# A second quarter of the MLP's second layer by Strassen's seven products, on the same four PSUM banks

## The chip, the core and the metric

The kernel runs on one core of one Trainium2 chip. The metric is the device time of one execution in microseconds, less being better; 2064.8 us is the median of three runs before the change (2063.86 to 2065.09).

## The reference, cut to what matters

One layer of a hybrid encoder trunk on 256 tokens with 2048 features: two token mixers, a cross-attention, a squared-ReLU MLP with 8192 hidden units, and a final RMSNorm. The change touches the MLP's second layer, the product with `w_ff2`.

```python
D_MODEL = 2048; SEQ = 256; D_FF = 4 * D_MODEL
...
    h = rms_norm(x, norm_ffn_g[l])
    x = x + jnp.square(jax.nn.relu(h @ w_ff1[l])) @ w_ff2[l]
return rms_norm(x, norm_final_g)
```

## The kernel before, in words

All matrix products are made to nearly fp32 precision from three products of rounded parts: a weight tile `raw` that a DMA brings is rounded by ScalarE (ACT) to `whi`, VectorE (DVE) makes the remainder `wlo = raw - whi`, and TensorE (PE) multiplies hi by hi, hi by lo and lo by hi. Activations are kept as such pairs as well (a `Quad` `q` holds four K-tiles of 128 hidden units for all 256 tokens).

The MLP runs in four feature blocks (`fb` 0 to 3) of 2048 hidden units. In a block, `blocks` computes the first layer in eight steps `b2` of 256 hidden units (256 columns of `w_ff1`; two transfers of 1 MB each), and after each second step one of the block's four quads `hid[q]` is complete. The second layer then adds the block's share to the result `res` (2 row tiles of 128 tokens, 2048 columns, here four quarters `n` of 512 columns). Quarters 1, 2 and 3 are made by `chunk`: four pieces, one for each quad `q`, each with one 1 MB transfer of a 512 x 512 piece of `w_ff2`, its `whi`/`wlo` in two halves, and 24 matmuls of 512 columns; the two PSUM banks `s0`, `s1` are added to `res` when the fourth piece is done (L1098).

Quarter 0 is made by Strassen's scheme (`seven_products`, L1014 to L1043): a 512 x 512 piece of weights is taken as two K-halves `i`, each with four sub-blocks of 128 x 256. DVE forms sums of the sub-blocks (`tt`, L1021 to L1023); ACT and DVE make the hi and lo parts of seven matrices for one half (`sh`, `sl`, L1029 and L1030); PE multiplies them with seven combinations of the hidden units (`q` itself or the sums `cm` that `mixes` makes) in 21 matmuls of 256 columns (L1041 to L1043). The seven results stay in four PSUM banks (`seven`, tile name `b`) over all four quads and all four blocks. After the last, `unmix` copies the banks to `pc` and DVE adds them to quarter 0 of `res`.

The buffers matter here. `raw` has three buffers, shared by classical and seven-product pieces. `whi` and `wlo` have four each (two pieces). `sh` and `sl` have one each: the second half of a piece can be written only when PE has read the first.

Within an engine the instructions run in the order of the built program. A scheduler makes that order from the program's order and from priorities: transfers and the making of `whi`, `wlo`, `tt`, `sh`, `sl` have a high one, so they stand early; the rest follows as its inputs are due. All weight transfers are issued from SP's queue, in its order, each when its `raw` buffer is free.

Of the kernel before, what the change touches and what calls it, by code (L numbers as in the profile page):

```python
# [50 lines left out]
def trunk(ctx: ExitStack, tc: tile.TileContext, x, mem, positions, norm_mix_g, w_in, conv_w, gdn_a_log, gdn_dt_bias,  # L51
# [67 lines left out]

    def chunk(quads, pieces_of, evac, before=None, hold=None, between=None):  # L120


# [4 lines left out]
        held = {q: fetch(pieces_of(q), 4, 512, hold=hold) for q in ((2, 3) if hold else ())}

        def products(q, i, part, halves):
            t, c0, c1, o = part  # L130
# [4 lines left out]
            pe.matmul(o, xh, wl, start=False, stop=False)  # L135
            pe.matmul(o, xl, wh, start=False, stop=last)  # L136
# [876 lines left out]

    def seven_products(both, cm, src, first, last):  # L1014

        raw = wp.tile([P, 2048], F32, name="raw", tag="raw", bufs=3)
        rv = raw.rearrange("p (i x c) -> p i x c", i=2, x=4)
        tt = fp.tile([P, 2, 4, 256], F32, name="tt", tag="tt", bufs=1)
        with tc.high_priority(offset=100000):
            nc.sync.dma_start(raw.rearrange("p (k n) -> p k n", k=4), src.rearrange("(k p) n -> p k n", p=P))  # L1020
            vec.tensor_add(tt[:, :, 0:2, :], rv[:, :, 0:1, :].to_broadcast([P, 2, 2, 256]), rv[:, :, 1:3, :])  # L1021
            vec.tensor_add(tt[:, :, 2, :], tt[:, :, 1, :], rv[:, :, 1, :])
            vec.tensor_add(tt[:, :, 3, :], tt[:, :, 2, :], rv[:, :, 3, :])  # L1023
        for i in range(2):
            with tc.high_priority(offset=100000):
                sh, sl = (fp.tile([P, 7 * 256 + ROOM], F32R, name=n, tag=n, bufs=1)[:, SHIFT:SHIFT + 7 * 256]
                          .rearrange("p (x c) -> p x c", x=7) for n in ("sh", "sl"))
                for xs, src in ((slice(0, 3), rv[:, i, 1:4, :]), (slice(3, 7), tt[:, i])):
                    act.activation(sh[:, xs, :], src, AF.Copy)  # L1029
                    vec.tensor_sub(sl[:, xs, :], src, sh[:, xs, :].bitcast(F32))  # L1030
# [13 lines left out]

    def unmix():

        pc = fp.tile([P, 8, 256], F32, name="pc", tag="tt", bufs=1)
        for g in range(4):
            n = 2 if g < 3 else 1
            act.activation(pc[:, 2 * g:2 * g + n, :], seven[g].rearrange("p (a c) -> p a c", a=2)[:, :n, :], AF.Copy)  # L1050
        c12, c11, c22, c21 = (res[:, t, c * 256:(c + 1) * 256] for t in range(NT) for c in range(2))
# [14 lines left out]
    for fb in range(4):  # L1066
        hid, mixed = [], []

        def strassen(q):
            seven_products(hid[q].both, mixed[q], w_ff2[0, fb * D + q * 512:fb * D + (q + 1) * 512, 0:512],  # L1070
                           fb == 0 and q == 0, fb == 3 and q == 3)

        for b2 in range(8):
            if b2 % 2 == 0:
                hid.append(quad_a())
                hs = fp.tile([P, 4, S], F32, name="hs", tag="hs", bufs=2)
            at = slice(b2 % 2 * 2, b2 % 2 * 2 + 2)
# [15 lines left out]
        for n in range(1, 4):
            ns = slice(n * 512, (n + 1) * 512)
# [6 lines left out]
            def evac_o(t, ps, c0, c1):  # L1101
                got = add(t, ps, 0, 512)
                if fb == 3:
                    square_sum(ssq4[:, t, n:n + 1], got)
                    vec.tensor_mul(got, got, gfin[:, ns])

            def evac_last(t, ps, c0, c1):
# [18 lines left out]
                if t == 0:  # L1126
                    vec.tensor_mul(res[:, t, ns], res[:, t, ns], gfin[:, ns])
                for c in (0, 3, 1, 2):
                    cs = slice(c * 512, (c + 1) * 512)
                    o = res[:, t, cs]  # L1130
                    if t and c == 3:
                        vec.scalar_tensor_tensor(o, o, r, gfin[:, cs], op0=ALU.mult, op1=ALU.mult)
# [24 lines left out]

# [26 lines left out]
```

## Time and profile before

| | |
|---|---|
| median of three runs | 2064.8 us |
| the profiled execution's own time | 2066.05 us |
| its span in the profile | 2064.3 us |
| the MLP's blocks 0, 1 and 2 (1419.20 to 1592.66 and the next two) | 173.46, 173.43, 173.44 us |
| the rest of the last block and the end (from 1939.53) | 124.77 us |
| DVE busy in a block of 173.46 us | 122.45 us |
| ACT busy in it | 90.69 us |
| mean granted TensorE clock | 0.999 |

The profile is of one execution; its span lies 1.75 us under that execution's own time, which in turn is 1.25 us over the median of the runs. Busy times of an engine are the union of its instructions' times. A matmul's recorded time overlaps that of the next one, so its pace is read from start to start. "Idle before" is time in which the engine waited for the named instruction or transfer. All stretches are in microseconds from the start of the span.

### The profile page before, as it was taken

The numbers are of one execution on the slowest core, as the hardware profiler recorded it, in microseconds if no ns is written. First come the engines' busy times: TensorE is split into PE (matmuls) and PEld (weight loads), VectorE is DVE, ScalarE is ACT, GpSimd is POOL, SyncE is SP. The second block draws the span as 40 slices with busy tenths as digits, with TensorE's granted clock in tenths as the row PEclk, the third lists the DMA queues.
The fourth block names the chain that finished last, engine by engine and source line by source line (L and its number), as shares of the span: only waits on it lengthen the run. The fifth ranks groups of instructions, "written<-read, shape, count | busy, mean of one in ns | idle before, by whom it ended". The sixth has DMA issues, their size and how long they took to land.

```text
span 2064.3 us, 29089 instructions
## 1 busy us (share of the span) xinstructions
PE 2045.1 (99%) x11240; PEld 1774.0 (86%) x11240; DVE 1510.3 (73%) x2381; ACT 1132.2 (55%) x1669; POOL 26.9 (1%) x37
## 2 busy tenths in 40 slices
PE   8999999999999999999999999999999999999998
PEld 6888888888888888888888898888888888988887
DVE  6785888588957896688767665768758756775885
ACT  7564664556445644565456555555546545554664
POOL 0000000000000000000000000000000000000000
PEclk9999999999999999999999999999999999999999
DMA  8797655465556555655567664565656566656653
GB/s 302 229 313 233 207 192 199 164 208 181 198 183 199 183 195 189 189 182 180 189 192 234 194 193 147 182 189 181 224 184 198 179 204 194 194 194 195 192 198 129
DMA packets 328313, 408.28 MB, mean 198 GB/s; under 512 B 31200, under 2 KB 236528, under 8 KB 328048
## 3 DMA queue, kind: packets, MB, share of 16 engines
q1 hardware_dynamic: 328032, 405.92, 61.0%
q8 instruction: 88, 1.44, 0.3%
q10 hardware_dynamic: 144, 0.52, 0.1%
q14 instruction: 49, 0.40, 0.1%
HBM read 391.19 MB, written 15.22 MB: 197 GB/s over the span
## 4 chain that ended last, share of the span: by engine, by line
PE 97%; DMA 1%; SPq 1%; issue 0%; DVE 0%; ACT 0%; POOLq 0%; POOL 0%; DVEq 0%; ACTq 0%
PE s L172 34%; PE s L174 17%; PE s L135 12%; PE s L134 12%; PE s L136 12%; PE b L1041 1%; PE b L1042 1%; PE b L1043 1%; PE b L689 1%; DMA xc<-x 1%; PE b L590 1%; PE b L104 0%; PE b L105 0%; PE b L106 0%; SPq L290 0%
## 5 line engine op out<-in xcount | busy, mean ns | idle before, releaser
L94 DVE TENSOR_TENSOR wlo<-raw,whi 128x1024 fp32r<-128x1024 f32 x668 | 816.0, 1223 | 412.6 <-ACT whi L93 405.7
L93 ACT ACTIVATE whi<-raw 128x1024 fp32r<-128x1024 f32 x668 | 706.6, 1060 | 689.1 <-PE s L172 331.2
L172 PE MATMUL s<-q,whi 128*128 128x512 f32 x3072 | 959.7, 392 | 2.2 <-DVE bo L187 2.1
L174 PEld LDWEIGHTS s<-q,wlo 128*128 128x128 f32 x3072 | 575.3, 188 | 123.6
L174 PE MATMUL s<-q,wlo 128*128 128x256 f32 x3072 | 611.9, 280 | 0.0
L172 PEld LDWEIGHTS s<-q,whi 128*128 128x128 f32 x3072 | 468.8, 188 | 5.2 <-DVE bo L187 2.5
L134 PE MATMUL s<-whi,q 128*128 128x512 f32 x1136 | 443.6, 392 | 0.7 <-ACT whi L93 0.7
L135 PE MATMUL s<-wlo,q 128*128 128x512 f32 x1136 | 443.5, 390 | 0.6 <-DVE wlo L94 0.6
L136 PE MATMUL s<-whi,q 128*128 128x512 f32 x1136 | 441.8, 390 | 0.0
L135 PEld LDWEIGHTS s<-wlo,q 128*128 128x128 f32 x1136 | 213.9, 188 | 43.5 <-DVE wlo L94 1.1
L134 PEld LDWEIGHTS s<-whi,q 128*128 128x128 f32 x1136 | 213.7, 188 | 42.9 <-ACT whi L93 1.1
L136 PEld LDWEIGHTS s<-whi,q 128*128 128x128 f32 x1136 | 213.3, 188 | 42.8 <-DVE q L257 0.2
L541 DVE SCALAR_TENSOR_TENSOR acc<-bo,cw,acc 128x255 f32<-128x255 f32 (+1 forms) x144 | 61.3, 479 | 3.3 <-ACT acc L538 3.0
L1029 ACT ACTIVATE sh<-raw 128x768 fp32r<-128x768 f32 x32 | 27.1, 847 | 49.1 <-DMA raw<-w_ff 32.5
L187 DVE TENSOR_TENSOR bo<-bo,s 128x256 f32<-128x256 f32 x128 | 47.9, 415 | 0.0
L649 DVE TENSOR_TENSOR pr<-lw,tw 32x31 f32<-32x31 f32 (+15 forms) x124 | 40.2, 324 | 8.7 <-DMA lw<-scr_l 7.1
L651 DVE TENSOR_TENSOR tw<-tw,pr 32x31 f32<-32x31 f32 (+15 forms) x124 | 40.5, 327 | 2.2
L186 ACT ACTIVATE bo<-s 128x256 f32<-128x256 f32 x128 | 41.0, 370 | 0.0
L1030 DVE TENSOR_TENSOR sl<-tt,sh 128x1024 fp32r<-128x1024 f32 x32 | 39.1, 1223 | 0.0
L1029 ACT ACTIVATE sh<-tt 128x1024 fp32r<-128x1024 f32 x32 | 33.6, 1051 | 8.4 <-DVE tt L1023 8.4
L1043 PE MATMUL b<-sh,cm 128*128 128x256 f32 x128 | 35.5, 279 | 0.0
L1042 PE MATMUL b<-sl,cm 128*128 128x256 f32 x128 | 35.5, 279 | 0.0
(359 smaller groups left out, 1575.5 us busy)
## 6 DMA issues: line engine op xcount, KB each, us to landing
raw<-w_in SPq DMA_DIRECT2D x143, 1024.0 KB, 5.1
raw<-w_ff SPq DMA_DIRECT2D x128, 1024.0 KB, 5.8
raw<-w_xkv SPq DMA_DIRECT2D x31, 1024.0 KB, 6.4
raw<-w_out SPq DMA_DIRECT2D x16, 1024.0 KB, 5.9
raw<-w_xq SPq DMA_DIRECT2D x16, 1024.0 KB, 5.4
raw<-w_xo SPq DMA_DIRECT2D x16, 1024.0 KB, 5.4
dec_d<-dec_w SPq DMA_DIRECT2D x8, 384.0 KB, 7.9
dec<-dec_d SPq DMA_DIRECT2D x8, 384.0 KB, 4.2
```

The source lines that it names most:

```text
L93: act.activation(hi, src, AF.Copy)
L94: vec.tensor_sub(lo, src, hi.bitcast(F32))
L134: pe.matmul(o, xh, wh, start=first, stop=False)
L135: pe.matmul(o, xh, wl, start=False, stop=False)
L136: pe.matmul(o, xl, wh, start=False, stop=last)
L172: pe.matmul(ps[b], wh[:, b * P:(b + 1) * P], xhl, start=kk == 0, stop=False)
L174: pe.matmul(ps[b][:, :S], wl[:, b * P:(b + 1) * P], xh, start=False, stop=kk == KT - 1)
L187: vec.tensor_add(o, o, ps[b][:, :S])
L541: vec.scalar_tensor_tensor(acc[:, d:], ps[:, :S - d], cw[:, j, blk:blk + 1], acc[:, d:], op0=ALU.mult, op1=ALU.add)
L1029: act.activation(sh[:, xs, :], src, AF.Copy)
L1042: pe.matmul(o, lhs[0], sl[:, x, :], start=False, stop=False)
L1043: pe.matmul(o, lhs[1], sh[:, x, :], start=False, stop=last and i == 1 and (m % 2 == 1 or m == 6))
```

## The change

In blocks 0, 1 and 2, quarter 1 is made by the seven products too; its classical chunk falls away there. In block 3 quarters 1 to 3 stay classical. Both quarters use the same four banks in turn: in each of the blocks 0 to 2 the banks gather quarter 0 over the block's four quads, are copied out, cleared and added to `res` (`unmix(0, True)`), and then gather quarter 1, with a second `unmix(1, True)`. So `unmix` runs seven times in place of once. The pieces are hung behind the classical pieces of quarters 2 and 3 by a new argument `behind` of `chunk`. S(q,n) names the seven-product piece of quad q in quarter n, C(n,q) a classical piece. The program's order is: S(0,0), S(1,0) in the first layer as before, then S(2,0); C(2,0), S(3,0), C(2,1), unmix, C(2,2), S(0,1), C(2,3), S(1,1); C(3,0), C(3,1), S(2,1), C(3,2), S(3,1), C(3,3), unmix.

Beside this, `cm` has four buffers in place of two, `hs` one in place of two, one of the four sums is written back into `raw`, and the final gain (1 MB, broadcast to all partitions) is loaded in block 3 in two halves into buffers of `cb` and `hs` rather than before the MLP. The banks are cleared by ACT (a copy with scale 0), not by DVE.

```diff
-    def chunk(quads, pieces_of, evac, before=None, hold=None, between=None):
+    def chunk(quads, pieces_of, evac, before=None, hold=None, between=None, behind={}):
...
+                for f in behind.get(q, ()):
+                    f()
...
+    def clear():
+        for g in range(4):
+            act.activation(seven[g].rearrange("p (a c) -> p a c", a=4), ident.unsqueeze(1).to_broadcast([P, 4, P]),
+                           AF.Copy, scale=0.0)
...
-        cm = fp.tile([P, 2, 2, 4, P], F32R, name="cm", tag="cm", bufs=2)
+        cm = fp.tile([P, 2, 2, 4, P], F32R, name="cm", tag="cm", bufs=4)
...
-            vec.tensor_add(tt[:, :, 2, :], tt[:, :, 1, :], rv[:, :, 1, :])
-            vec.tensor_add(tt[:, :, 3, :], tt[:, :, 2, :], rv[:, :, 3, :])
+            vec.tensor_add(rv[:, :, 0, :], tt[:, :, 1, :], rv[:, :, 1, :])
+            vec.tensor_add(tt[:, :, 2, :], rv[:, :, 0, :], rv[:, :, 3, :])
...
-                for xs, src in ((slice(0, 3), rv[:, i, 1:4, :]), (slice(3, 7), tt[:, i])):
+                for xs, src in ((slice(0, 4), rv[:, i]), (slice(4, 7), tt[:, i])):
...
-    def unmix():
+    def unmix(n, again):
...
+            if again:
+                clear()
...
-                hs = fp.tile([P, 4, S], F32, name="hs", tag="hs", bufs=2)
+                hs = fp.tile([P, 4, S], F32, name="hs", tag="hs", bufs=1)
...
-        if fb == 3:
-            strassen(2)
-        for n in range(1, 4):
+        strassen(2)
+        if fb == 3:
+            load_gfin()
+        for n in range(1 if fb == 3 else 2, 4):
...
             chunk(hid, cols(w_ff2[0, fb * D:(fb + 1) * D, :], n * 512), evac_last if last else evac_o,
-                  hold=quad_b if last else None)
-            if n < 3 and fb < 3:
-                strassen(n + 1)
+                  hold=quad_b if last else None,
+                  behind=({} if fb == 3 else
+                          {0: (step(3, 0),), 1: (lambda: unmix(0, True),), 2: (step(0, 1),), 3: (step(1, 1),)} if n == 2 else
+                          {1: (step(2, 1),), 2: (step(3, 1),)}))
+            if n == 3 and fb < 3:
+                unmix(1, True)
```

How the built order changes is shown at three places of block 0. The numbers in names tell buffers' uses apart.

On SP's queue, in the second layer: L83 fetches a classical piece, L1020 (before) and L1035 (after) a seven-product piece. Before, from the last piece of quarter 1 to the piece after quarter 2:

```order
L83 DMA raw_14026<-w_ff2 128x4x512
L1020 DMA raw_14062<-w_ff2 128x4x512
L83 DMA raw_14124<-w_ff2 128x4x512
L83 DMA raw_14158<-w_ff2 128x4x512
L83 DMA raw_14192<-w_ff2 128x4x512
L83 DMA raw_14226<-w_ff2 128x4x512
L1020 DMA raw_14262<-w_ff2 128x4x512
```

After, from C(2,2) (raw_14130) to C(3,2) (raw_14450); raw_14164 is S(0,1), raw_14224 C(2,3), raw_14258 S(1,1), raw_14322 and raw_14356 C(3,0) and C(3,1), raw_14390 S(2,1):

```order
L83 DMA raw_14130<-w_ff2 128x4x512
L1035 DMA raw_14164<-w_ff2 128x4x512
L83 DMA raw_14224<-w_ff2 128x4x512
L1035 DMA raw_14258<-w_ff2 128x4x512
L83 DMA raw_14322<-w_ff2 128x4x512
L83 DMA raw_14356<-w_ff2 128x4x512
L1035 DMA raw_14390<-w_ff2 128x4x512
L83 DMA raw_14450<-w_ff2 128x4x512
```

Seven-product pieces now stand between the classical ones with one or two of these between them, where four stood before.

On DVE, before, around the end of a classical chunk (L1098 adds its two banks to `res`) and the two halves of a seven-product piece (`sl_14069` the first, `sl_14096` the second):

```order
L94 TENSOR_TENSOR wlo_14127<-raw_14124,whi_14126 128x1024
L1030 TENSOR_TENSOR sl_14069<-tt_14063,sh_14068 128x1024
L94 TENSOR_TENSOR wlo_14131<-raw_14124,whi_14130 128x1024
L94 TENSOR_TENSOR wlo_14161<-raw_14158,whi_14160 128x1024
L1098 TENSOR_TENSOR res_10093<-s0_13922,res_10093 128x512
L1098 TENSOR_TENSOR res_10093<-s1_13923,res_10093 128x512
L94 TENSOR_TENSOR wlo_14165<-raw_14158,whi_14164 128x1024
L1030 TENSOR_TENSOR sl_14096<-raw_14062,sh_14095 128x768
L1030 TENSOR_TENSOR sl_14096<-tt_14063,sh_14095 128x1024
```

After, at the end of n=2's chunk (L1120 is the add, `wlo_14325` and `wlo_14329` are C(3,0), L1071 and L1072 the recombination), and then at S(0,1) (`sl_14171`, `sl_14198`) and S(1,1) (`tt_14259`, `sl_14265`), up to C(3,2)'s first `wlo`:

```order
L1071 TENSOR_TENSOR pc_14110<-pc_14110 128x256
L1072 TENSOR_TENSOR res_10093<-res_10093,pc_14110 128x256
L94 TENSOR_TENSOR wlo_14325<-raw_14322,whi_14324 128x1024
L1120 TENSOR_TENSOR res_10093<-s0_13980,res_10093 128x512
L94 TENSOR_TENSOR wlo_14329<-raw_14322,whi_14328 128x1024
L1120 TENSOR_TENSOR res_10093<-s1_13981,res_10093 128x512
```

```order
L1045 TENSOR_TENSOR sl_14171<-raw_14164,sh_14170 128x1024
L1045 TENSOR_TENSOR sl_14171<-tt_14165,sh_14170 128x768
L1045 TENSOR_TENSOR sl_14198<-raw_14164,sh_14197 128x1024
L1045 TENSOR_TENSOR sl_14198<-tt_14165,sh_14197 128x768
L1036 TENSOR_TENSOR tt_14259<-raw_14258 128x2x512
L1037 TENSOR_TENSOR raw_14258<-tt_14259,raw_14258 128x2x256
L1038 TENSOR_TENSOR tt_14259<-raw_14258 128x2x256
L1045 TENSOR_TENSOR sl_14265<-raw_14258,sh_14264 128x1024
L1045 TENSOR_TENSOR sl_14265<-tt_14259,sh_14264 128x768
L94 TENSOR_TENSOR wlo_14453<-raw_14450,whi_14452 128x1024
```

Before, classical work stood between the two halves of a piece; now both halves and the start of the next piece follow each other, and the add of a chunk stands ahead of the second `wlo` of the next chunk's first piece.

On PE, before, behind the last products of a first half (L1041 to L1043) comes a classical piece (L134 to L136):

```order
L1042 MATMUL b_13000<-sl_14069,cm_13657 128x256
L1043 MATMUL b_13000<-sh_14068,cm_13657 128x256
L134 MATMUL s0_14122<-whi_14126,q_13006 128x512
L135 MATMUL s0_14122<-wlo_14127,q_13006 128x512
L136 MATMUL s0_14122<-whi_14126,q_13006 128x512
```

After, behind the last products of S(0,1)'s first half (L1056 to L1058, `sh_14170`):

```order
L1057 MATMUL b_12998<-sl_14171,cm_13197 128x256
L1058 MATMUL b_12998<-sh_14170,cm_13197 128x256
L1056 MATMUL b_12995<-sh_14197,q_13004 128x256
L1056 MATMUL b_12996<-sh_14197,cm_13197 128x256
L1056 MATMUL b_12997<-sh_14197,cm_13197 128x256
L1056 MATMUL b_12998<-sh_14197,cm_13197 128x256
L1057 MATMUL b_12995<-sl_14198,q_13004 128x256
```

The second half (`sh_14197`, in the same buffer as `sh_14170`) follows at once, its four products that need `sh` alone first.

More of the change, by code (lines that the diff above doesn't have):

```diff
@@ L998, in trunk, with load_gfin, final_gain @@
     seven = [bank() for _ in range(4)]
-    for g in range(4):
-        vec.memset(seven[g], 0.0)
+    gfin = []
+    def load_gfin():
+        for i, tag in enumerate(("cb", "hs")):
+            g = fp.tile([P, 1024], F32, name="gfin", tag=tag, bufs=1)
+            nc.sync.dma_start(g, norm_final_g[i * 1024:(i + 1) * 1024].partition_broadcast(P))
+            gfin.append(g)
+    def final_gain(c0, c1):
+        return gfin[c0 // 1024][:, c0 % 1024:c0 % 1024 + c1 - c0]
+    def clear():
[3 more added lines that the diff above has]
+    clear()
     def mixes(hs):
@@ L1017, in seven_products @@
         rv = raw.rearrange("p (i x c) -> p i x c", i=2, x=4)
-        tt = fp.tile([P, 2, 4, 256], F32, name="tt", tag="tt", bufs=1)
+        tt = fp.tile([P, 2, 3, 256], F32, name="tt", tag="tt", bufs=1)
         with tc.high_priority(offset=100000):
@@ L1036, in mix @@
                 return [cm[:, e, i, x, :] for e in range(2)]
-            for m, (lhs, x) in enumerate(((own(0, 0), 0), (own(1, 0), 2), (mix(3), 1), (own(1, 1), 6), (mix(1), 3),
-                                          (mix(2), 5), (mix(0), 4))):
+            for m, (lhs, x) in enumerate(((own(0, 0), 1), (own(1, 0), 3), (mix(3), 2), (own(1, 1), 6), (mix(1), 4),
+                                          (mix(2), 0), (mix(0), 5))):
                 o = seven[m // 2][:, m % 2 * 256:m % 2 * 256 + 256]
@@ L1043, in seven_products @@
                 pe.matmul(o, lhs[1], sh[:, x, :], start=False, stop=last and i == 1 and (m % 2 == 1 or m == 6))
-    def unmix():
[L1047 to L1051, printed above, removed]
+    def unmix(n, again):
+        pc = fp.tile([P, 7, 256], F32, name="pc", tag="tt", bufs=1)
+        with tc.high_priority(offset=50000):
+            for g in range(4):
+                m = 2 if g < 3 else 1
+                act.activation(pc[:, 2 * g:2 * g + m, :], seven[g].rearrange("p (a c) -> p a c", a=2)[:, :m, :], AF.Copy)
+            if again:
+                clear()
+        c12, c11, c22, c21 = (res[:, t, n * 512 + c * 256:n * 512 + (c + 1) * 256] for t in range(NT) for c in range(2))
         p1, p2, p3, p4, p5, p6, p7 = (pc[:, m, :] for m in range(7))
@@ L1067, in trunk, with strassen, step @@
         hid, mixed = [], []
-        def strassen(q):
-            seven_products(hid[q].both, mixed[q], w_ff2[0, fb * D + q * 512:fb * D + (q + 1) * 512, 0:512],
-                           fb == 0 and q == 0, fb == 3 and q == 3)
+        def strassen(q, n=0):
+            seven_products(hid[q].both, mixed[q], w_ff2[0, fb * D + q * 512:fb * D + (q + 1) * 512, n * 512:(n + 1) * 512],
+                           q == 0, q == 3)
+        def step(q, n):
+            return lambda: strassen(q, n)
         for b2 in range(8):
@@ L1104, in evac_o @@
                     square_sum(ssq4[:, t, n:n + 1], got)
-                    vec.tensor_mul(got, got, gfin[:, ns])
+                    vec.tensor_mul(got, got, final_gain(n * 512, n * 512 + 512))
             def evac_last(t, ps, c0, c1):
@@ L1126, in evac_last @@
                 if t == 0:
-                    vec.tensor_mul(res[:, t, ns], res[:, t, ns], gfin[:, ns])
+                    vec.tensor_mul(res[:, t, ns], res[:, t, ns], final_gain(n * 512, n * 512 + 512))
                 for c in (0, 3, 1, 2):
@@ L1131, in evac_last @@
                     if t and c == 3:
[L1132 removed]
+                        vec.scalar_tensor_tensor(o, o, r, final_gain(c * 512, c * 512 + 512), op0=ALU.mult, op1=ALU.mult)
                     elif t and c == 2:
@@ L1151, in trunk @@
             if fb == 3 and n == 2:
-                unmix()
+                unmix(0, False)
                 for t in range(NT):
@@ L1155, in trunk @@
                     square_sum(ssq4[:, t, 0:1], got)
-                    vec.tensor_mul(got, got, gfin[:, 0:512])
+                    vec.tensor_mul(got, got, final_gain(0, 512))
 _INS = ["x", "mem", "positions", "norm_mix_g", "w_in", "conv_w", "gdn_a_log", "gdn_dt_bias", "ret_gn_g", "gdn_norm_g",
```

2 lines of the change are left out of this document (removed).

## The prediction, made before the changed kernel was run

> **What bounds the kernel now.** I read the page first: its busy line and its chain say who sets the end. In the chain line every share is time on the path to the end.
>
> ```profile
> span 2064.3 us, 29089 instructions
> PE 2045.1 (99%) x11240; PEld 1774.0 (86%) x11240; DVE 1510.3 (73%) x2381; ACT 1132.2 (55%) x1669; POOL 26.9 (1%) x37
> PE 97%; DMA 1%; SPq 1%; issue 0%; DVE 0%; ACT 0%; POOLq 0%; POOL 0%; DVEq 0%; ACTq 0%
> ```
>
> TensorE sets the end. The view of stretches then gives one feature block of the MLP (columns: length, then busy time of PE, PEld, DVE, ACT, POOL, granted clock, DMA share, GB/s), and the view of lines in that block gives the prices.
>
> ```profile
> 1419.20:1592.66 173.46, 173.46 (x970) 151.46 (x969) 122.45 (x140) 90.69 (x108) 0.00 (x0) 1.00 0.61 194
> 1592.66:1766.09 173.43, 173.43 (x969) 151.43 (x969) 122.70 (x139) 90.94 (x108) 0.00 (x0) 1.00 0.60 194
> L94 DVE TENSOR_TENSOR wlo<-raw,whi 128x1024 fp32r<-128x1024 f32 x56 | 68.5, 1224 | 43.5 <-ACT whi L93 43.0
> L93 ACT ACTIVATE whi<-raw 128x1024 fp32r<-128x1024 f32 x56 | 59.2, 1058 | 64.1 <-PE s L136 27.5 <-PE s L172 27.2 <-DMA raw<-w_ff 9.3
> L1030 DVE TENSOR_TENSOR sl<-tt,sh 128x1024 fp32r<-128x1024 f32 x8 | 9.8, 1223 | 0.0
> L1029 ACT ACTIVATE sh<-tt 128x1024 fp32r<-128x1024 f32 x8 | 8.4, 1053 | 2.3 <-DVE tt L1023 2.3
> L1030 DVE TENSOR_TENSOR sl<-raw,sh 128x768 fp32r<-128x768 f32 x8 | 7.6, 952 | 1.0 <-ACT sh L1029 1.0
> L1029 ACT ACTIVATE sh<-raw 128x768 fp32r<-128x768 f32 x8 | 6.8, 847 | 13.5 <-DMA raw<-w_ff 9.7 <-PE b L1043 3.8
> L1021 DVE TENSOR_TENSOR tt<-raw 128x1024 f32<-128x1024 f32 x4 | 4.9, 1224 | 6.2 <-DMA raw<-w_ff 6.2
> L1098 DVE TENSOR_TENSOR res<-s,res 128x512 f32<-128x512 f32 x6 | 3.8, 682 | 0.0
> L1022 DVE TENSOR_TENSOR tt<-tt,raw 128x512 f32<-128x512 f32 x4 | 2.7, 683 | 0.0
> ```
>
> PE is busy for all of a block. ACT mostly waits for PE (64.1 us), so buffers are full and the weights are early; but 9.3 + 9.7 + 6.2 us are already waits for a weight transfer.
>
> **What PE saves.** Start times of matmuls give their real pace, since a busy time overlaps the next one.
>
> ```profile
> 1479.72 0.39 PE L135 MATMUL s<-wlo,q 128*128 128x512 f32 x1
> ...
> 1481.31 0.39 PE L136 MATMUL s<-whi,q 128*128 128x512 f32 x1
> 1481.54 0.28 PE L1042 MATMUL b<-sl,q 128*128 128x256 f32 x1
> ...
> 1483.77 0.28 PE L1043 MATMUL b<-sh,cm 128*128 128x256 f32 x1
> ```
>
> Seven steps of 512 columns take 1.59 us, 0.227 each; nineteen of 256 take 2.23, 0.117 each. A classical piece (4 K-tiles x 2 row tiles x 3) is 24 x 0.227 = 5.45 us, a seven-product piece 2 x 21 x 0.117 = 4.91. Twelve pieces change (three blocks, four quads): 12 x 0.54 = 6.5 us less PE.
>
> **What is added off PE.** Per piece, DVE does 2 x (1.22 + 0.95) + 1.22 + 2 x 0.68 = 6.9 us instead of 2 x 1.22 = 2.4, ACT 2 x 1.90 = 3.8 instead of 2.1. Per block two recombinations come on top.
>
> ```profile
> L1050 ACT ACTIVATE pc<-b 128x512 f32<-128x512 f32 (+1 forms) x4 | 2.0, 535 | 0.1
> L1054 DVE TENSOR_TENSOR res<-res,pc 128x256 f32<-128x256 f32 x1 | 0.4, 426 | 0.0
> ```
>
> Each is 4 x 0.54 on ACT, four clears of a bank that I price the same, and 11 x 0.42 = 4.6 us on DVE. A block's DVE goes from 122.5 to 122.5 + 4 x 4.5 + 9.2 - 2 x 0.68 = 148 us of about 171: no bound over the block. But from the start of n=2 to the end of its chunk (four classical pieces, three seven-product ones, one recombination, two adds) DVE needs 4 x 2.4 + 3 x 6.9 + 4.6 + 1.4 = 36.3 us and PE 4 x 5.45 + 3 x 4.91 = 36.5. No reserve builds up there. The half with four of the seven matrices first, cm in four buffers, hs in one (its next write comes a whole b2, 11 us, later), the clear on ACT, and the gain vector loaded in block 3 in two halves I cost at 0: no PE row waits for them; the cover of the last is the two raw buffers ahead, and without it 1 MB, 4.9 us, would show.
>
> **The one pair sh/sl and the three raw buffers.** These rows price a hand-over from the first half of a piece to its second, and a transfer.
>
> ```profile
> 1510.50 0.28 PE L1043 MATMUL b<-sh,cm 128*128 128x256 f32 x1
> ...
> 1510.82 0.85 ACT L1029 ACTIVATE sh<-raw 128x768 fp32r<-128x768 f32 x1 [1.41 <-PE b L1043]
> ...
> 1511.70 0.96 DVE L1030 TENSOR_TENSOR sl<-raw,sh 128x768 fp32r<-128x768 f32 x1 [1.03 <-ACT sh L1029]
> ...
> 1512.65 1.23 DVE L1030 TENSOR_TENSOR sl<-tt,sh 128x1024 fp32r<-128x1024 f32 x1
> DMA to landing us min/median/max: 4.9/5.8/5.9
> 1485.14 0.37 SPq L83 DMA_DIRECT2D raw<-w_ff  x1
> 1486.01 0.37 SPq L1020 DMA_DIRECT2D raw<-w_ff  x1
> 1492.90 1.23 DVE L1021 TENSOR_TENSOR tt<-raw 128x1024 f32<-128x1024 f32 x1 [0.76 <-DMA raw<-w_ff]
> 1510.69 2.36 SPq L83 DMA_DIRECT2D raw<-w_ff  x2
> ```
>
> sh is rewritten 0.32 us after the last matmul of the half starts, and sl 0.88 after that. A transfer takes 4.9 (alone) to 5.9 us, and 6.9 when another was issued 0.9 before it (1486.01 to 1492.90). The seven-product raw issued at 1486.01 is held until the second half's sl has read it (1512.66), 27 us. Before, one is held at a time and classical pieces cycle on two buffers. In the order after, raw_14164 and raw_14258, the next two seven-product pieces, are fetched ahead of raw_14322 and raw_14356 (n=3's first two classical pieces) and held together, so classical pieces cycle on one. And PE has nothing between the halves of S(0,1), nor between it and S(1,1) (S(q,n): quad q, quarter n; C(n,q): classical piece).
>
> **The sum of the waits.** I follow the order through one block; E is where PE starts C(3,0), and I work with cross-engine hand-overs of 0.05.
> 1. C(3,1). raw_14322 can go when S(3,0)'s second half has read its raw: that half's predecessor ends on PE 9.9 us before E (24 + 9 matmuls and a half of 2.46 stand between), plus 0.32 + 1.06 + 1.23 gives E-7.4. With 5.4 for a transfer partly shared it lands at E-2.0; whi 1.06, wlo 1.22, then, in DVE's order, the add of n=2's result (0.60), then the second wlo (1.22): E+2.1. Only then is raw_14356 issued (it stands at the head of SP's queue, raw_14390 and raw_14450 behind it): 4.9, whi 1.06, 0.1: E+8.15. PE is through C(3,0) at E+5.45: wait 2.7, and 0.8 more for wlo (1.22 + 0.05, less two products). 3.5.
> 2. PE finishes C(3,1) and half a piece at E+16.85. S(0,1)'s second half: sl is ready 0.32 + 1.09 + 1.23 + 0.05 = 2.69 after the last matmul's start, and four sh products hide 0.47 of that: wait 2.1, done at E+21.45.
> 3. S(1,1): its sums stand behind that sl on DVE: from E+19.4, sl 0.95, tt 1.22, 0.72, then sh 1.1, sl 1.28 gives E+24.65: wait 2.7.
> 4. C(3,3): eight more products, two and nine bring PE to the end of S(1,1)'s first half at E+27.1; its transfer waits for the second half's sl (0.22 + 1.1 + 1.23 later, E+29.65); 5.8 (another was issued 1.5 before) and 1.1: E+36.6. PE is there at E+34.55 (22 x 0.227 + 2.46): wait 2.05, and 0.8 for wlo. 2.85.
> 5. The next block's first and second w_ff1 transfers follow on the same chain (wlo to issue, 5.8, whi, wlo): 1.45 and 1.85.
>
> Together 14.4 us a block, 43 in three. After that the third buffer is back. Ends: the hand-over of 2.1 in steps 2 and 3 alone, 4.2 a block, is forced by the order; with all five transfers at 6.9 instead of 5.4, 4.9, 5.8, 5.8, 5.8 it is 21.2. I take 14.4, since step 1's longest link and 4's are rows of this stretch and not ends. The profiled execution took 2066.05 us (span 2064.3), 1.25 above the median. 2066.05 - 6.5 + 43.3 = 2102.9, on the median's scale 2101. Ends 2064.8 - 6.5 + 12.6 = 2071 and 2064.8 - 6.5 + 63.6 = 2122.
>
> [...]
>
> **Rivals.**
> - PE stays fed and the kernel is faster: 2064.8 - 6.5 = 2058. For it: PE waits nowhere in the blocks before, with one pair sh/sl and raws already held for 27 us. It wins if a block's waits stay under 2.2 us. Against it: the forced 4.2.
> - Only steps 2 and 3 show and the raw chain hides under PE (if transfers are issued earlier than I count): 2064.8 - 6.5 + 3 x 4.8 = 2073.
> - The clock falls in the waits. These stretches at the end show PE idle for 3.0 us at full grant and then half:
>
> ```profile
> 2056.00:2059.00 3.00, 0.00 (x0) 0.00 (x0) 2.16 (x6) 1.26 (x2) 0.55 (x1) 1.00 0.55 207
> 2059.00:2064.00 5.00, 0.00 (x0) 0.00 (x0) 0.00 (x0) 0.08 (x1) 0.00 (x0) 0.50 0.53 210
> ```
>
> My waits are 2.1 to 2.7 at a stretch, just under. If the three longest of each block tripped it, and half pace lasted as long as the idle that caused it, 9 x 1.5 = 13.5 us more: 2115. [...]
>
> **How the numbers follow.** Forecast 0.78 (its own range 2084 to 2114), only the hand-overs 0.07, the clock 0.06, PE fed 0.06, and 0.03 for waits that just cancel the saving. Within 0.2% (4 us, about what a measurement of this kernel can tell) there is only that last case. The range 2074 to 2114 leaves out the fed case, the cancelling one, and half of the two other rivals.
>
> **What would show it.** The stretches of blocks 0 to 2 grow from 173.4 to about 185 us, the last one stays near 124.8; PE's busy share falls and PE gets rows that wait for whi and wlo of w_ff2 (2 to 3 us each) and for sh/sl at the head of S(0,1)'s second half and of S(1,1). ACT's whi shows waits for w_ff transfers well above 9.3 us a block. The count of PE matmuls rises by 12 x 18 = 216. Wrong would be: blocks of 171 us with no PE wait (the first rival), waits of PE for sh/sl alone, or waits named for the bank clears or the recombination, which I cost at nothing beside their place in DVE's row.

## The result, and the profile after

The changed kernel takes 2112.5 us (median of four runs, 2111.9 to 2115.1) against 2064.95 us for the kernel before on the same chip: a ratio of 1.0233 with a 95% interval of 1.0216 to 1.0251, 47.6 us slower. The forecast was 2101 in a range of 2074 to 2114, so the time lies in the range, 11.5 us above the forecast. One of the eleven runs of e9 below took 2910.63 us at a granted clock of 0.655; it is left out of the median given for e9.

The page of the changed kernel, its busy line and its chain:

```profile
span 2110.2 us, 29727 instructions
PE 2061.7 (98%) x11456; PEld 1786.4 (85%) x11456; DVE 1574.9 (75%) x2497; ACT 1169.8 (55%) x1745; POOL 26.9 (1%) x37
PE 90%; DMA 5%; DVE 2%; ACT 2%; SPq 1%; issue 0%; POOLq 0%; POOL 0%; ACTq 0%; DVEq 0%
```

In the chain PE has 90% where it had 97%, and DMA has 5%, DVE and ACT 2% each: the path to the end now runs through transfers and through the making of hi and lo parts. 11456 - 11240 = 216 matmuls more, as the change has it. PE's busy time *grew*, from 2045.1 to 2061.7 us, although its work shrank; this is a first hint of the clock, which accounts for a part of it. The view of stretches by block (length, busy time of PE, PEld, DVE, ACT, POOL, granted clock, DMA share, GB/s):

```profile
1419.20:1606.00 186.80, 175.94 (x1013) 152.69 (x1013) 140.23 (x173) 98.67 (x127) 0.00 (x0) 0.97 0.55 177
1606.00:1794.00 188.00, 178.49 (x1036) 155.03 (x1035) 144.90 (x180) 101.98 (x132) 0.00 (x0) 0.98 0.55 178
1794.00:1983.00 189.00, 178.09 (x1046) 155.05 (x1045) 144.77 (x179) 102.97 (x133) 0.00 (x0) 0.99 0.55 180
```

A block takes some 187 to 189 us where it took 173.4, and the granted clock is below 1. The waits stand in the timeline of PE, here in block 0 (start, length, instruction, and in brackets the idle time before it and what ended it). S(q,n) is the seven-product piece of quad q and quarter n, C(n,q) the classical one, as in the prediction:

```profile
1491.97 0.73 PE L134 MATMUL s<-whi,q 128*128 128x512 f32 x2 [2.42 <-ACT whi L93]
1493.23 0.79 PE L135 MATMUL s<-wlo,q 128*128 128x512 f32 x1 [0.53 <-DVE wlo L94]
1502.38 0.50 PE L135 MATMUL s<-wlo,q 128*128 128x512 f32 x1 [0.50 <-DVE wlo L94]
1511.33 0.38 PE L1056 MATMUL b<-sh,q 128*128 128x256 f32 x1 [1.15 <-ACT sh L1044]
1517.38 0.39 PE L1056 MATMUL b<-sh,q 128*128 128x256 f32 x1 [1.19 <-ACT sh L1044]
1531.21 0.73 PE L134 MATMUL s<-whi,q 128*128 128x512 f32 x2 [2.41 <-ACT whi L93]
1532.47 0.50 PE L135 MATMUL s<-wlo,q 128*128 128x512 f32 x1 [0.53 <-DVE wlo L94]
```

These are C(3,0), C(3,1), S(0,1)'s second half, S(1,1)'s first half, and C(3,3). Comparing every start-to-start distance in the three blocks with the usual one of the same kind of matmul gives the account of the lost time: 38.5 us of waits (13.5, 11.5 and 13.5 by block), 8.5 us lost where matmuls ran at half pace (products of 512 columns start 0.427 us apart there, 0.227 at full clock), and 6.1 us in gaps too small to name, 53.1 us together. 2064.95 - 6.5 (PE's saving) + 53.1 = 2111.6; measured 2112.5. How the 53.1 us are split depends a little on the size from which a gap is called a wait; the row of waits is an account, not a measurement of each cause.

Half pace shows in five stretches of the blocks, 20.5 us in all; here are the two in block 0 and what stands ahead of each:

```profile
1489.20:1492.60 3.40, 0.98 (x4) 0.30 (x2) 0.65 (x1) 1.74 (x2) 0.00 (x0) 1.00 0.02 8
1492.60:1496.00 3.40, 2.87 (x8) 2.20 (x8) 3.30 (x6) 3.40 (x8) 0.00 (x0) 0.50 0.01 2
1496.00:1499.40 3.40, 3.40 (x10) 2.62 (x9) 3.33 (x9) 0.15 (x1) 0.00 (x0) 0.50 0.94 304
1509.70:1513.10 3.40, 2.00 (x13) 1.39 (x12) 1.79 (x2) 1.79 (x2) 0.00 (x0) 1.00 0.00 0
1513.10:1516.50 3.40, 3.09 (x15) 2.79 (x14) 2.92 (x4) 0.22 (x1) 0.00 (x0) 0.50 0.79 267
```

Two things are to be seen: after 3.4 us in which PE was busy for only 0.98 or 2.00 us the clock was 0.50 for at least the next 3.4 us; and at 1489.2 to 1496.0, while PE waits for C(3,0) and then starts on it, the DMA engines stand all but still (share 0.01 to 0.02). The bandwidth is there; no `raw` buffer is free. The next transfer, C(3,1)'s, is issued at 1494.93, just behind the second `wlo` of C(3,0) (its row in DVE's timeline, at 1493.69 for 1.22 us, is shown at e6), which is the last to read the buffer that it needs.

### The profile page after: what moved, and what is told of

Its sections match the earlier page's. It is cut to its first block, busy times and chain, and to the rows that moved or that the text cites. A ratio compares the mean times of both kernels' runs of the same rounds, so it can differ in the third digit from the quotient of the medians.

```text
span 2110.2 us, 29727 instructions
## 1 busy us (share of the span) xinstructions
PE 2061.7 (98%) x11456; PEld 1786.4 (85%) x11456; DVE 1574.9 (75%) x2497; ACT 1169.8 (55%) x1745; POOL 26.9 (1%) x37
## 4 chain that ended last, share of the span: by engine, by line
PE 90%; DMA 5%; DVE 2%; ACT 2%; SPq 1%; issue 0%; POOLq 0%; POOL 0%; ACTq 0%; DVEq 0%
PE s L174 33%; PE s L176 17%; PE s L135 10%; PE s L134 10%; PE s L136 10%; DMA raw<-w_ff 4%; PE b L1057 2%; PE b L1058 2%; PE b L1056 2%; DVE wlo L94 1%; PE b L691 1%; ACT whi L93 1%; ACT sh L1044 1%; DMA xc<-x 1%; PE b L592 1%; DVE sl L1045 1%
## 5 line engine op out<-in xcount | busy, mean ns | idle before, releaser
L94 DVE TENSOR_TENSOR wlo<-raw,whi 128x1024 fp32r<-128x1024 f32 x644 | 783.9, 1222 | 369.3 <-ACT whi L93 360.6
L134 PE MATMUL s<-whi,q 128*128 128x512 f32 (+1 forms) x1040 | 406.6, 396 | 12.0 <-ACT whi L93 12.0
L135 PE MATMUL s<-wlo,q 128*128 128x512 f32 (+1 forms) x1040 | 409.0, 393 | 4.8 <-DVE wlo L94 4.7
L136 PE MATMUL s<-whi,q 128*128 128x512 f32 (+1 forms) x1040 | 406.0, 392 | 0.0
L134 PEld LDWEIGHTS s<-whi,q 128*128 128x128 f32 x1040 | 196.3, 190 | 53.0 <-ACT whi L93 14.7
L136 PEld LDWEIGHTS s<-whi,q 128*128 128x128 f32 x1040 | 196.4, 189 | 39.3
L1044 ACT ACTIVATE sh<-raw 128x1024 fp32r<-128x1024 f32 x56 | 59.1, 1055 | 63.8 <-PE b L1058 32.3
L1045 DVE TENSOR_TENSOR sl<-raw,sh 128x1024 fp32r<-128x1024 f32 x56 | 68.4, 1221 | 23.8 <-ACT sh L1044 23.4
L1058 PE MATMUL b<-sh,cm 128*128 128x256 f32 x224 | 61.5, 284 | 0.0
L1056 PE MATMUL b<-sh,cm 128*128 128x256 f32 x224 | 55.8, 285 | 1.4 <-ACT sh L1044 1.4
L1056 PE MATMUL b<-sh,q 128*128 128x256 f32 x168 | 48.4, 288 | 8.3 <-ACT sh L1044 8.3
L1045 DVE TENSOR_TENSOR sl<-tt,sh 128x768 fp32r<-128x768 f32 x56 | 53.3, 952 | 0.0
L1057 PE MATMUL b<-sl,q 128*128 128x256 f32 x168 | 48.6, 290 | 0.1
L1058 PE MATMUL b<-sh,q 128*128 128x256 f32 x168 | 48.0, 286 | 0.0
```

What stands on the lines that cost most here:

```text
L94: vec.tensor_sub(lo, src, hi.bitcast(F32))
L1056: pe.matmul(o, lhs[0], sh[:, x, :], start=first and i == 0 and m % 2 == 0, stop=False)
L1057: pe.matmul(o, lhs[0], sl[:, x, :], start=False, stop=False)
L1058: pe.matmul(o, lhs[1], sh[:, x, :], start=False, stop=last and i == 1 and (m % 2 == 1 or m == 6))
```

## The experiments

The theory going in: two shortages (three `raw` buffers, one pair `sh`/`sl`) add up their waits, the clock comes on top, and DVE's added work costs nothing. Each experiment takes one of these away. The times of each group of experiments stand against runs of the kernel before that were made with it on the same chip.

### e1, e2, e3, e4: room for the pair, for the raws, for both

Room is made by cutting `cm` from four buffers to two (e1 is that alone; in e4 to one). In all four kernels pieces multiply with the sums of another quad: the same work with other numbers.

```diff
# e1
-        cm = fp.tile([P, 2, 2, 4, P], F32R, name="cm", tag="cm", bufs=4)
+        cm = fp.tile([P, 2, 2, 4, P], F32R, name="cm", tag="cm", bufs=2)
-  seven_products(hid[q].both, mixed[q], ...
+  seven_products(hid[q].both, mixed[q if n == 0 else 2 + q % 2], ...
# e2: e1 and
-  sh, sl = (fp.tile([P, 7 * 256 + ROOM], F32R, name=n, tag=n, bufs=1) ...
+  sh, sl = (fp.tile([P, 7 * 256 + ROOM], F32R, name=n, tag=n, bufs=2) ...
# e3: e1 and, in seven_products
-        raw = wp.tile([P, 2048], F32, name="raw", tag="raw", bufs=3)
+        raw = fp.tile([P, 2048], F32, name="raw7", tag="raw7", bufs=2)
# e4: cm bufs=1, raw7 bufs=1, sh/sl bufs=2
```

> Control for the next three: cm gets two buffers instead of four, which frees 16 KB a partition; for this, S(0,1) and S(1,1) multiply with the sums of quads 2 and 3 instead of their own (same work, other numbers). TensorE's instructions keep their order. All theories: the time of the changed kernel, 2112.5 within 4 us, with the same waits. If it is faster by more than 4, the four cm buffers themselves cost something, which no theory here has.

> e1 with two pairs of sh/sl instead of one; the three raw buffers stay. Theory (waits come from two shortages, the raw ring and the single pair; the clock falls come on top of the waits): the hand-over waits at S(0,1) and S(1,1) go (1.15 + 0.23 + 1.19 + 0.23 = 2.8 us a block in the trace of the changed kernel), and the half-pace stretches that follow them (3 of 3.4 us, 1.7 us lost in each, 5 in all): 2112.5 - 8.4 - 5 = 2099; the raws are then free about 2 us earlier too, which would give up to 6 more: 2093. The waits for whi at C(3,0) and C(3,3) stay. Rival (the pair is the root and the ring is only held long because of it): nearly all waits go, 2065 or less. Rival (DVE's added work sets the pace; the waits are only where it shows): DVE's work is the same, 2112.

> e1 with two raw buffers of their own for seven-product pieces, the three shared ones left to classical pieces; the single pair sh/sl stays. In the built order classical pieces now run ahead and S(1,1) to S(3,1) stand among the next block's first-layer matmuls, so the hand-overs get work between them as well. Theory (raw ring first): the waits for whi and wlo at C(3,0), C(3,1), C(3,3) and the next first-layer pieces go (7.2 us a block, 21.5 in three) and with them half-pace stretches of 10 us (5 us lost): 2086 at most; if the new order also covers the hand-overs, 2112.5 - 13 x 3 - 8.5 = 2065, and 2058 if nothing is left. Rival (hand-over on the pair is the root): 8.4 + 5 us of it stay, and not more than 15 us are gained: 2097 or above. Rival (DVE's work): 2112.

> Both relieved at once: two pairs sh/sl, one raw buffer of its own for seven-product pieces and three for classical ones (cm gets one buffer, so all pieces of a block multiply with one quad's sums: same work, other numbers). Theory: no wait of the ring and none of the pair, 2058 to 2065; one raw alone makes each seven-product piece fetch only after the piece ahead has been read, and if this shows, one wait of 2 to 4 us a block stays: 2070. Rival (DVE's work, 148 us in 171, with the recombination in the stretch where it is due): 2100 to 2112, with PE waiting for sl and wlo behind DVE that never idles.

Measured, beside 2064.96 us for before: e1 2115.8 (ratio 1.0245, 1.0230 to 1.0261), e2 2060.1 (0.9976, 0.9966 to 0.9986), e3 2059.3 (0.9972, 0.9961 to 0.9982), e4 2058.0 (0.9966, 0.9953 to 0.9979).

The control holds within its 4 us (3.3 above the changed kernel). Then comes the surprise: *either* relief alone removes nearly all of it (e2 and e3 lie 2.1 and 1.3 us above e4). The two-pair kernel was expected at 2093 to 2099 by the theory; the rival "the pair is the root and the ring is only held long because of it" had 2065 or less, and was right for it. But the own raws, with one pair, do as much: for e3 the last branch of its theory holds (2058 if the new order covers the hand-overs and nothing is left), and e4 lies in its theory's 2058 to 2065. The rival that DVE's work sets the pace (2100 to 2112) falls in all three. Two stretches by block and the chain of e2, and then, from its view of waits between 1460 and 1990, the row for ACT (line, what it waits for: total, times, longest); last, the first block of e3:

```profile
1419.20:1590.20 171.00, 171.00 (x1037) 152.57 (x1036) 143.01 (x176) 103.36 (x132) 0.00 (x0) 1.00 0.61 194
1590.20:1761.20 171.00, 171.00 (x1036) 152.57 (x1036) 144.41 (x179) 103.42 (x132) 0.00 (x0) 1.00 0.61 198
PE 97%; DMA 1%; SPq 1%; issue 0%; DVE 0%; ACT 0%; POOLq 0%; POOL 0%; DVEq 0%; ACTq 0%
ACT whi L93 <- DMA raw<-w_ff: 52.8, 23, 4.2
...
1419.20:1590.20 171.00, 171.00 (x1040) 152.65 (x1039) 142.78 (x177) 103.35 (x133) 0.00 (x0) 1.00 0.61 196
```

PE is busy for all of each 171 us, at full clock. In e2 ACT still waits 52.8 us for transfers (123.8 us in the changed kernel, in the same stretch): the ring of three is still short, but with two pairs the pieces are made early enough that nothing on PE waits. DVE's work (143 to 144 us a block) is no bound over the block either. So the waits of the two shortages don't add; they are links of one ring: a half of `sh`/`sl` waits for PE to finish the half before, its `raw` is held until then, the next classical piece waits for that `raw`, and PE, which waits for that piece, is late with the next half. Cut it at the pair or at the raws and PE stays fed. One thing these runs leave together: with the buffers the built order of PE changes too (in e2 S(0,1) is mixed into C(3,0), in e3 S(1,1) and later pieces stand among the next block's first-layer matmuls). In e2's trace the halves of a piece still follow each other directly (up to 42 seven-product matmuls in a row), so there it is the second pair and not work put between the halves that removes the hand-over; in e3's trace no two halves follow each other (never more than 21), so e3 alone can't tell the raws from the order. e7 changes the order alone.

### e5: the waits filled, for the clock

```diff
+                for m in range(warm if q == 0 else 0):
+                    pe.matmul(ps[0], quads[0][0][:, m % 4, 0:P], quads[0].both[:, m % 4, :], start=True, stop=True)
...
+    def fill(k):
+        for m in range(k):
+            pe.matmul(seven[3][:, 256:512], h3[0].both[:, m % 4, 0:P], h3[0].both[:, m % 4, 0:256], start=False, stop=False)
```

> The changed kernel with idle matmuls where TensorE waits longest in blocks 0 to 2: 8 of 512 columns ahead of C(3,0) (8 x 0.227 = 1.8 us, into the bank that C(3,0) starts afresh), 8 of 256 columns between the halves of S(0,1) (0.93) and 4 ahead of S(1,1) (0.47), these into a half bank that nothing reads. All other instructions keep their order, so transfers and hand-overs stay as they are and the waits grow shorter by what is put into them. Theory (the half-pace stretches are caused by TensorE standing still): they vanish or nearly so, 8.5 us less by the accounting of the changed kernel's trace (20.4 us at half pace), less 1.5 us where the filling is longer than the wait: 2104 to 2106. Rival (the clock falls for another reason, or one short wait is enough): 2112 to 2114, with half-pace stretches as before.

Measured: 2115.9 us (before 2065.3; ratio 1.0244, 1.0229 to 1.0259). The time that the theory expected, 2104 to 2106, was not met; it is nearer to the rival's 2112 to 2114, and half pace shows in 30.7 us in place of 20.5. Two rows from the timeline of PE and three stretches show why:

```profile
1493.12 0.50 PE L135 MATMUL s<-wlo,q 128*128 128x512 f32 x1 [0.41 <-DVE wlo L94]
1500.98 0.73 PE L134 MATMUL s<-whi,q 128*128 128x512 f32 x2 [2.58 <-ACT whi L93]
...
1492.80:1496.20 3.40, 3.08 (x14) 2.55 (x15) 3.29 (x6) 3.25 (x7) 0.00 (x0) 1.00 0.15 13
1499.60:1503.00 3.40, 1.49 (x5) 0.96 (x6) 2.43 (x4) 2.19 (x3) 0.00 (x0) 1.00 0.00 0
1503.00:1506.40 3.40, 3.40 (x9) 2.64 (x9) 3.40 (x4) 1.72 (x2) 0.00 (x0) 0.50 0.36 87
```

At C(3,0) the filling did what it was for: only 0.41 us of wait and full clock there, where the changed kernel had 6.8 us at half. But C(3,1)'s weights come when they come: PE, done with C(3,0) sooner, now waits 2.58 us for them in place of 0.50, and the clock falls there. Over the three blocks e5 has 30.7 us of waits, 9.7 of filling, 11.9 lost to the clock, 4.7 of small gaps: 57.0 against 53.1. At this place time at half pace and waiting time replace each other, because the transfers set the pace: C(3,1) starts its `wlo` products at 1502.24 here and at 1502.38 in the changed kernel. So the 8.5 us of the account need not be 8.5 us that a steady clock would give back; no run here has these waits at a steady clock. The built order was to stay as it was; from C(3,3) of block 0 on it does not quite (168 of the 11456 places in PE's order hold another matmul), so the totals of the later blocks compare less well than this first place.

### e6: the recombination's DVE work left out

```diff
     def unmix(n, again):
...
+        if again:
+            return
         vec.tensor_add(p2, p1, p2)
```

> The changed kernel without the eleven DVE operations of each recombination in blocks 0 to 2 (six recombinations of 11 x 0.42 = 4.6 us; the banks are still copied out and cleared, so quarters 0 and 1 lack their sums from these blocks). Theory (the single pair makes the seven-product pieces late, they hold the raws, DVE itself has room): the waits stay, 2112 within 4. Rival (the added DVE work sits in the stretch without reserve and pushes the pieces): up to 4.6 us of wait a block and the clock losses behind it go, 2092 to 2099.

Measured: 2095.2 us (before 2065.3; ratio 1.0142, 1.0127 to 1.0157), 17 us less than the changed kernel; waits in the three blocks fall from 38.5 to 25.9 us and the clock's loss from 8.5 to 3.2. The rival is right here. The timeline of DVE in the changed kernel has the first two of the eleven operations at 1487 and the other nine between C(3,0)'s `wlo` and the sums (L1036) of S(0,1):

```profile
1491.95 1.23 DVE L94 TENSOR_TENSOR wlo<-raw,whi 128x1024 fp32r<-128x1024 f32 x1 [3.81 <-ACT whi L93]
...
1493.69 1.22 DVE L94 TENSOR_TENSOR wlo<-raw,whi 128x1024 fp32r<-128x1024 f32 x1
...
1495.42 0.42 DVE L1073 TENSOR_TENSOR pc<-pc 128x256 f32<-128x256 f32 x1
...
1498.42 0.42 DVE L1081 TENSOR_TENSOR res<-res,pc 128x256 f32<-128x256 f32 x1
1498.87 1.23 DVE L1036 TENSOR_TENSOR tt<-raw 128x1024 f32<-128x1024 f32 x1
```

and in e6 the sums start 5.0 us earlier:

```profile
1492.09 1.22 DVE L94 TENSOR_TENSOR wlo<-raw,whi 128x1024 fp32r<-128x1024 f32 x1
1493.22 0.68 DVE L1122 TENSOR_TENSOR res<-s,res 128x512 f32<-128x512 f32 x1
1493.83 1.22 DVE L1036 TENSOR_TENSOR tt<-raw 128x1024 f32<-128x1024 f32 x1
```

Of these 5.0 us the nine operations take 3.4; the rest is that C(3,0)'s second `wlo` itself comes 1.6 us earlier. DVE is not full (it had waited 3.81 us just ahead of this); it is a link of the ring there, and what is put on it late makes S(0,1) late. One thing is not taken apart: without the eleven operations the built order shifts too. From C(3,1) of block 0 on ACT makes S(0,1)'s `sh` ahead of C(3,1)'s `whi`, and 295 of the 11456 places in PE's order hold another matmul. The 17 us belong to the DVE work and to that shift together.

### e7 and e8: another place in the program, and finer raws

e7 keeps every buffer of the changed kernel and moves pieces (`late` is the `strassen` of the block before); e8 keeps the places in the program and splits `raw`.

```diff
# e7
-  {0: (step(3, 0),), 1: (lambda: unmix(0, True),), 2: (step(0, 1),), 3: (step(1, 1),)} if n == 2 else
-  {1: (step(2, 1),), 2: (step(3, 1),)}
+  {0: (step(3, 0),), 1: (lambda: unmix(0, True),), 3: (step(0, 1),)} if n == 2 else
+  {2: (step(1, 1),)}
...
+            if late and b2 in (0, 2):
+                late(2 + b2 // 2, 1)
+                if b2 == 2:
+                    unmix(1, True)
...
             if n == 3 and fb < 3:
-                unmix(1, True)
+                late = strassen
# e8
-        raw = wp.tile([P, k * n], F32, name="raw", tag="raw", bufs=3)
+            raws = [wp.tile([P, k * n // 2], F32, name="raw", tag="raw", bufs=6) for _ in range(2)]
```

> The same computation and buffers as the changed kernel (one pair, three raws, four cm), only other places in the program: S(0,1) behind C(2,3), S(1,1) behind C(3,2), S(2,1) and S(3,1) with the recombination of quarter 1 among the next block's first-layer steps (behind b2 = 0 and b2 = 2). In the built order each half then has 1 to 5 us of other matmuls ahead of it. Theory (what costs is that TensorE has nothing between the halves and pieces while one pair and few raws are held): 2058 to 2062, faster than before by 0.1 to 0.3%. Rival (five raws' worth of demand on three buffers stays whatever the order): some of the waits for whi come back at the next block's first-layer pieces, 2070 to 2090. Rival (DVE's work): no gain, 2105 to 2112.

> The changed kernel with raw in six buffers of 512 KB (two K-tiles each, two transfers a piece, everywhere in the kernel) instead of three of 1 MB; a seven-product piece makes its sums half by half (six DVE operations of half the size instead of three) and gives its first half's buffer back one half earlier. One pair sh/sl. Theory: the ring is longer by about one half buffer, so the waits for whi shrink; the hand-overs stay unless the built order covers them: 2065 to 2090. Rival (the pair alone counts): the waits at S(0,1) and S(1,1) stay whole, and so do the others, 2105 or more. More and smaller transfers may cost or gain a few us in the 1375 us ahead of the MLP as well; its trace tells them apart.

Measured (before 2065.3): e7 2065.6 (1.0000, 0.9991 to 1.0010), e8 2084.9 (1.0093, 1.0078 to 1.0108). With the order alone 47 of the 53 us of the account go: one pair and three raws are nearly enough if the pieces stand far apart. Neither number on record was met, the theory's 2058 to 2062 nor the first rival's 2070 to 2090; what is left is of the rival's kind but smaller: 5.0 us of waits at the head of the next block, and no half pace. ACT's waits between 1500 and 1545, and PE's rows of block 0's turn to block 1:

```profile
ACT whi L93 <- DMA raw<-w_ff: 19.9, 4, 7.4
...
1531.04 0.51 PE L176 MATMUL s<-q,wlo 128*128 128x256 f32 x2 [0.30 <-DVE wlo L94]
1539.63 0.74 PE L174 MATMUL s<-q,whi 128*128 128x512 f32 x2 [0.83 <-ACT whi L93]
1540.89 0.50 PE L176 MATMUL s<-q,wlo 128*128 128x256 f32 x2 [0.52 <-DVE wlo L94]
```

e8 gives 28 us by a finer ring at the old places in the program; 19.3 us of waits and 5.0 of clock remain in its trace. Its built order moved with the buffers: the changed kernel has a run of 52 seven-product matmuls in each block, e8 never more than 21 in a row. So e8 doesn't show how much of the 28 us is the finer ring and how much is work put between the halves. It lies within its theory's 2065 to 2090, and its rival (the pair alone counts, 2105 or more) falls.

### e9 to e12: a version faster than both, and its control

e9 is e7 with b2 in (1, 3) for (0, 2); e10 is e7 with e8's half raws; e11 is e9 with them; e12 is the kernel *before* with them.

> e7 with S(2,1) and S(3,1) behind b2 = 1 and b2 = 3 of the next block instead of 0 and 2, so that S(1,1)'s and S(2,1)'s raws are not held together while the first pieces of w_ff1 come. Theory (the 5.0 us of waits that e7's trace has left, at 1530 to 1540, 1705 to 1714 and 1885 to 1887, are the raw ring at the head of a block: ACT waits 19.9 us for w_ff transfers between 1500 and 1545, 7.4 at the longest): they go, 2058 to 2061. Rival (the ring is short there whatever is behind b2 = 0, since S(0,1) and S(1,1) are bunched ahead of it): 2064 to 2066. Rival (two pieces close to S(0,0) of the next block move the same wait to b2 = 4): 2063 to 2068, with waits there.

> e7 with the six half raw buffers of e8. Theory: a seven-product piece gives half of its raw back one half earlier, and whi can start on the first half of a transfer; e7's remaining 5.0 us of waits go: 2058 to 2061. Rival (the half transfers wait as long, since the second half is held to the end all the same): 2064 to 2066. e8's stretches ahead of the MLP show PE busy as before (692.9 of 700 us, 673.8 of 675), so no loss from there.

> e9 and e10 together. Theory: nothing is left to wait for, 2058 to 2060, the time of the two-pair kernel e2 and of e4 (2060.1 and 2058.0) within 2 us. Rival: if e9's order makes new waits at b2 = 4, they show here too, 2062 or more.

> Control for e10: the kernel before (quarter 0 alone by seven products) with the six half raw buffers. Theory (its TensorE waits nowhere in the blocks, so finer buffers have nothing to give there; the gain of e10 is the 6.5 us of matmul time that the seven products save): 2064 to 2066, the same as before, and 6 to 8 us above e10's 2058.0. Rival (the half buffers themselves speed the stretches ahead of the MLP up): 2057 to 2061, and then e10 owes its gain to them and the seven products of quarter 1 bring nothing.

Measured: e9 2062.5 (0.9986, 0.9977 to 0.9995), e10 2058.0 (0.9964, 0.9950 to 0.9977), e11 2058.0 (0.9965, 0.9952 to 0.9977), beside 2065.5 for before; e12 2063.35 (0.9989, 0.9980 to 0.9998) beside 2065.55. In e9's trace only 0.7 us of waits is left, as its theory said, but its median lies 1.5 us above the theory's range, and under the rivals'; its profiled execution, at 2061.0, was its fastest, and where the others lose 0.7 to 3.7 us more stays open. e10 and e11 meet their theories' 2058. Both compute all of the reference, as e2 to e4 do not, and they are the fastest that do, 7.5 us under before. The first block and the chain of e10:

```profile
1419.20:1590.20 171.00, 171.00 (x1038) 152.54 (x1037) 142.72 (x200) 99.89 (x129) 0.00 (x0) 1.00 0.62 194
PE 99%; DMA 0%; issue 0%; ACT 0%; DVE 0%; SPq 0%; POOLq 0%; POOL 0%; ACTq 0%
```

The control splits its gain. e12 misses both of its numbers by a little: 2063.35 is 0.65 us under the 2064 to 2066 that it was to keep, and 5.4 us above e10 in place of 6 to 8. Taken so, 2.2 us of e10's gain are the half raws' (0.1%, at the edge of what is measured; where they arise stays open) and 2063.35 - 2057.99 = 5.4 us the seven products', where the prediction had priced the matmuls saved at 6.5. The two were timed on two chips, on which the kernel before differs by 0.1 us.

## Why the prediction was right, and where it was not

The direction and the main mechanism held: PE's saving of 6.5 us (5.4 by e10 against e12, 7.0 by e4 against before) is real and lost several times over in waits on transfers held back and on the single pair. The nearness of the number is in part luck: the waits alone come to 2064.95 - 6.5 + 38.5 = 2097, and what brings the time to 2112.5, near the upper end of 2114, are the clock and the small gaps, which the likeliest case had at nothing. By its own steps, in us a block:

| step | forecast | measured in blocks 0, 1, 2 |
|---|---|---|
| C(3,0) | 0 | 3.6, 1.9, 1.6 |
| 1. C(3,1) | 3.5 | 0.7, 1.8, 3.3 |
| 2. S(0,1), second half | 2.1 | 1.7, 1.7, 1.7 |
| 3. S(1,1) | 2.7 | 1.9, 2.4, 2.6 |
| 4. C(3,3) | 2.85 | 3.3, 2.0, 1.8 |
| 5. next first-layer pieces | 3.3 | 2.3, 1.7, 2.5 |
| sum | 14.4 | 13.5, 11.5, 13.5 |

- **C(3,0) was to start without a wait** because its transfer was taken at 5.4 us. The timeline of SP's queue shows it issued as the first of the two at 1481.98, 7.4 us before PE was through with the chunk of n=2, as the prediction had reckoned, but 1.4 us behind S(1,1)'s own transfer, and ACT starts on it at 1490.86:

```profile
1480.62 0.37 SPq L1035 DMA_DIRECT2D raw<-w_ff  x1
1481.98 13.32 SPq L83 DMA_DIRECT2D raw<-w_ff  x2
1490.86 2.01 ACT L93 ACTIVATE whi<-raw 128x1024 fp32r<-128x1024 f32 x2 [3.64 <-DMA raw<-w_ff]
```

  That is 8.9 us, where the prediction's slowest row had 6.9. The wait that this makes at C(3,0) is in part taken from C(3,1)'s, which is why the sum hardly moved. The forecast's own range begins at 2084, and no run shows the faster transfers that this end takes: in the two kernels' traces the fastest transfer of 1 MB into `raw` landed after 4.7 us (before) and 4.8 (changed), and this one took 8.9 behind another.
- **The clock.** The prediction made it a rival of its own, at 0.06 and with 13.5 us, instead of a term on top of its likeliest case. It came: 20.5 us at half pace and 8.5 us lost, most of the 11.5 us by which the forecast was short. Together with 6.1 us of small gaps and 4.8 us less of waits than forecast that is 9.8 of the 11.5. It took half pace to last as long as the idle that caused it; it lasted 3.41 us after 2.06 to 2.8 us of idle time, and 6.83 us once, after 2.8 (below).
- **The recombination "at nothing beside their place in DVE's row".** Wrong in size: without its DVE work the kernel is 17 us faster (e6). The average of DVE over the block (forecast 148, measured 140 to 145 us) was about right and said nothing on it; the prediction had even counted the stretch without reserve (36.3 us of DVE in 36.5 of PE) and did not ask where in DVE's row the recombination stands: ahead of S(0,1)'s sums.
- **The ends of the range.** "The hand-over of 2.1 in steps 2 and 3 alone, 4.2 a block, is forced by the order" was taken as a floor for the change. e3, e7 and e10 keep the single pair and show no wait at it, since the built order puts other matmuls between the halves. It held for this kernel's order only. The bounds of 2071 and 2122 still enclosed the time.
- **Waits added up as independent terms.** They were one ring: a relief takes away far more than its own terms. Those of the pair (steps 2 and 3) were 4.8 us a block, 14.4 in three, and e2 gained 52.4; those of the raws (steps 1, 4 and 5) were 9.65 a block, 29 in three, and e3 gained 53.2.
- **Two small slips.** Of the 64.1 us that ACT idles before `whi` in a block of the kernel before, the row names PE for 54.7, not for all. And 2102.9 less 1.25 is 2101.65, so on the median's scale the sum was nearer to 2102 than to 2101. Neither changes the argument.

The rival "PE fed, 2058" is what e4 then measured, 2058.0 (and e10 and e11, with finer raws): the price was right, the condition was not met by the change as it was made.

## What to carry to other kernels

When two short resources wait for each other (here a scratch pair that PE must release and a transfer ring that the scratch's input holds), don't sum their waits: look for the cheapest link to cut, and try the program's order before buffers. An engine that is far from full over a block (DVE here, 140 to 145 us of 187 to 189) can still be the late link in one stretch, so price added work at the place where it stands in that engine's row. A faster sequence on paper is worth trying at another place before it is dropped: the same change, spread over the next block and with finer transfers, is 0.36% faster than before rather than 2.3% slower.

## What the runs showed of the hardware that was not expected

In these traces the clock fell by a grid in time, not by the length of a wait. In the five kernels that show half pace inside the blocks (the changed one, e1, e5, e6, e8) every such stretch started at a whole multiple of 3.413 us from the first one of its run, and lasted 3.41 us, or 6.83. In the changed kernel they start at 1492.62, 1513.10, 1683.76, 1707.66 and 1895.39, which are 6, 50, 7 and 55 steps apart. These times are from the trace's own record of the granted clock. Cutting each run at this grid and taking PE's idle time in each piece from the starts of the matmuls: all 22 pieces at full clock with more than 2.05 us idle were followed by half pace; of those with less than 1.9 us none was; of the ten between, two were. In the changed kernel alone, the five pieces with 2.06, 2.20, 2.55, 2.8 and 2.8 us idle were followed by half pace, and no other in the blocks was; the most idle of these had 1.96 us. So a single wait of 2.6 us, counted from the starts, brought half pace or not by where it lay on the grid. The changed kernel's block 0 shows both. The 2.42 us ahead of 1491.97 (2.58 from the starts) and the small gaps beside it put 2.8 us of idle time into one piece, and half pace followed. The 2.41 us ahead of 1531.21 (2.57) were cut by an edge of the grid at 1530.16; the two pieces held 1.5 and, with the 0.53 us behind it, 1.95 us, and the clock stayed at full. What sets the step of 3.413 us is not shown.
